# Expert queries from the loaded float32 weights instead of from split halves, in a two-block model with 512 row gathers

## The chip, the cores and the metric

The kernel runs on one core of a Trainium2 chip. The metric is the device time of one execution in microseconds (us), the median of three runs. Times inside an execution are us from the start of the profiled span.

## The reference, cut to what matters

Two transformer blocks over 256 tokens of width 2048 (one core, float32). The change sits in the last stage, the expert layer of the second block:

```python
def peer(x, wq, keys1, keys2, u, v):          # x is rmsnorm(x, g) of the stream
    q = (xf @ wq).reshape(t, PEER_HEADS, PEER_QDIM)        # 2048 x 2048 product, 8 heads
    s1 = jnp.einsum('thd,kd->thk', q[..., :half], keys1)   # 128 keys each
    s2 = jnp.einsum('thd,kd->thk', q[..., half:], keys2)
    v1, i1 = lax.top_k(s1, 16)
    v2, i2 = lax.top_k(s2, 16)
    ...                                       # the best 16 of the 16 x 16 sums: top_s, expert
    gate = jax.nn.softmax(top_s)
    z = jnp.einsum('cd,ced->ce', xc, u[ec])   # 128 rows of u for each token
    act = jax.nn.gelu(z) * gc
    return jnp.einsum('ce,ced->cd', act, v[ec])  # 128 rows of v for each token
```

Each token picks 8 heads x 16 experts = 128 rows of `u` and 128 of `v`, 8 KB each.

## The kernel before

**The steps.** All weight products of the model are one list of `Step`s that `run` walks in order. A weight tile of 1 MB (`raw`, 3 buffers, loaded on SP's queue by `load`) serves two steps. For each step ACT writes `hi` (the weights rounded to fp32r, `split_hi`) and DVE writes `lo` (the rest, `split_lo`), up to four steps ahead; the activations are held as a pair `hi`, `lo` as well (class `XT`). A step of `unit_B` then issues 16 matmuls: 8 of `hi` against both halves of the activations (512 columns), 8 of `lo` against `hi` (256 columns).

**The rest of the work** is written as generators. `pump()` runs once after each step and lets every living generator go on to its next `yield`; so the place of each vector instruction between the steps is fixed when the program is written, and each engine works through its own list in that order.

**The queries** (`e_q` weights, tile `eq`). Eight heads, four steps each, 32 steps. At a head's end `leave` sums the two halves on DVE (`eq_u`), `e_query` multiplies by 1/rms (`stE.R`, a row vector that `norm_end` makes), PE multiplies by the keys (`esc`), ACT copies (`es`), and `e_route` finds the top 16 on DVE (`route`, some 45 small instructions and three of 128x800), writes the indices into `keys_slots`, and makes the gates (an Exp on ACT). The heads of token tile 0 are routed first, one after the other, and a head's routing begins only when nearly all of the `u` gathers of the head before are issued.

**The gathers.** `e_stream` handles 512 items: for each token tile (2), head (8) and rank (16) a "U" (rows of `u`) and a "V" (rows of `v`). POOL issues an indirect DMA of 128 rows, 1.05 MB, into a free row buffer. A U item is then one DVE instruction over 128x2048 with an accumulated sum; a V item is four PE matmuls into `vacc` with a diagonal matrix `dg_ring` that ACT makes. In each `pump()` at most one waiting item is taken, and its buffer goes back for the next gather. V items begin when all eight heads' queries are made (`Ee["q"] == EH`). Until then there are three row buffers (`rows_a`, in the tile "xt1"); then `wide_rows` adds the three weight buffers (`rows_w`) and three quarters of the tile "xt0" that held the activations `xE` (`rows_x`); one quarter of each of the tiles "xt1" and "xt0" holds the gain times x for a token tile (`gain_rows`, its input from `f_g` through ACT's queue).

Of the kernel before, what the change touches and what calls it, by code (L numbers as in the profile page):

```python
# [20 lines left out]
P = 128  # L21
# [35 lines left out]
class Step:  # L57
    def __init__(self, src, mm, ready=None, post=None, row=None):
        self.src, self.mm, self.ready, self.post, self.row, self.pre = src, mm, ready, post, row, None
# [3 lines left out]
def tile_model(ctx: ExitStack, tc: tile.TileContext, x, xT, par, a_in, a_out, kv_in, kv_f, b_in, b_out,  # L63
# [95 lines left out]
    def run(steps):  # L159
# [6 lines left out]
        nd = NRAW  # L166
        for i, st in enumerate(steps):
            while nl < min(i + LOOK_SPLIT + 1, 2 * i + 2, n):
                while nh < min(nl + 2, n):
# [4 lines left out]
                if nl % 2 == 0 and 2 * nd < n:  # L174
                    load(nd, steps)
                    nd += 1
# [5 lines left out]
            st.mm(his.pop(i), los.pop(i))  # L182
# [88 lines left out]

    class Late:
# [76 lines left out]
    def resid_norm(st, chunks_ready, xt, wn):  # L349

        for c in range(4):
# [3 lines left out]
            norm_chunk(st, c)  # L355
        yield
# [26 lines left out]
    def unit_B(src, xt, cb, name, nk=KT, inter=False, per_sub=False):  # L383
# [27 lines left out]
        def leave(i):  # L411
            def f():
                if per_sub:
                    u = uo = w4(f"{name}_u{i}", (P, 2, T))
                else:
                    if "u" not in box:
                        box["u"] = w4(f"{name}_u", (P, 4, T))
                    u = box["u"]
                    uo = u[:, 2 * i:2 * i + 2, :]
                V.tensor_reduce(uo, box[i].rearrange("p j (a t) -> p j t a", a=2), axis=AX.X, op=OP.add)  # L420
                if per_sub:
                    spawn(cb(i)(u))
                elif i == 1:
# [3 lines left out]
        for n, (i, kg) in enumerate(order):  # L427
            st = Step(src(n // 2), mm(i, kg), ready=lambda kg=kg: xt.done() > kg)
            if kg == ng - 1:
                st.post = leave(i)  # L430
            steps.append(st)
# [826 lines left out]
    xtE = Late("xE", "xt0")  # L1258
# [4 lines left out]
    def e_setup():  # L1263
# [12 lines left out]
        rows.extend([r4[:, i, :] for i in range(1, 4)])  # L1276
        yield
# [7 lines left out]
    def e_query(h):  # L1285

        def f(q):
# [12 lines left out]
            if h:  # L1300
                yield
# [262 lines left out]
```

## Time and profile before

| | |
|---|---|
| median of three runs | 3056.84 us (3056.22 to 3057.11) |
| the profiled execution | 3057.23 us, span 3055.5 us |
| PE, DVE, ACT, POOL busy | 87%, 66%, 33%, 25% of the span |
| DMA | 840.90 MB, mean 275 GB/s |
| mean granted TensorE clock | 0.975 |

The share of busy time is a mean over stages. From about 1650 us the program is in the expert stage; the views of the trace below are of that stage. "Busy" of DMA is the mean over the core's 16 DMA engines. A wait is put down to the engine that released it.

### The profile page before, as it was taken

What the parts mean: (1) busy time and instruction counts of PE and PEld (TensorE: products, weight loads), DVE (VectorE), ACT (ScalarE), POOL (GpSimd) and SP (SyncE); (2) the same over time, 40 slices, a digit from 0 to 9 for tenths busy, and PEclk for the clock granted to TensorE, in tenths of its full rate; (3) what the DMA queues carried; (4) which work ended last, traced back from release to release, by engine and by line L of the source; (5) the groups of instructions that cost most, each with busy time, mean ns of one, the idle gap of its engine ahead of it and who ended that gap; (6) DMA issues with size and microseconds to landing.
All of it is one profiled execution on the core that took longest, in us unless ns stands there. A gap on an engine that the chain in (4) does not pass through costs nothing.

```text
span 3055.5 us, 30995 instructions
## 1 busy us (share of the span) xinstructions
PE 2659.7 (87%) x11252; PEld 1852.1 (61%) x11252; DVE 2006.1 (66%) x3088; ACT 1019.2 (33%) x1595; POOL 777.9 (25%) x612
## 2 busy tenths in 40 slices
PE   8999999999999999999999658777777777777766
PEld 7888888888888888888888543233332223322222
DVE  7978765656666568777766886555555565655454
ACT  6545544655554444555455211100111111110000
POOL 0412110000000000000000244555554444444553
PEclk9999999999999999999999778999999999999999
DMA  7444545444445454454555789999999999999997
GB/s 257 152 146 154 175 159 184 167 154 172 173 155 183 169 181 158 171 179 162 184 180 194 272 315 407 421 422 421 421 421 422 421 421 422 419 421 421 421 421 309
DMA packets 118521, 840.90 MB, mean 275 GB/s; under 512 B 13152, under 2 KB 13536, under 8 KB 17376
## 3 DMA queue, kind: packets, MB, share of 16 engines
q0 software_dynamic: 73728, 536.90, 42.5%
q1 hardware_dynamic: 43920, 298.73, 28.0%
q10 hardware_dynamic: 720, 3.28, 0.3%
q8 instruction: 89, 1.46, 0.2%
q14 instruction: 64, 0.52, 0.0%
HBM read 836.77 MB, written 2.10 MB: 275 GB/s over the span
## 4 chain that ended last, share of the span: by engine, by line
PE 55%; DMA 25%; DVE 11%; issue 7%; POOL 2%; ACT 0%; POOLq 0%; DVEq 0%; ACTq 0%
DMA rows_w<-in_e_v_dram,keys_slots 6%; PE vacc L1433 6%; DMA rows_a<-in_e_v_dram,keys_slots 5%; DMA rows_x<-in_e_v_dram,keys_slots 4%; DMA rows_a<-in_e_u_dram,keys_slots 3%; DMA rows_w<-in_e_u_dram,keys_slots 3%; DMA rows_x<-in_e_u_dram,keys_slots 2%; DVE rows_a L1415 2%; PE dq L406 2%; PE az L406 2%; PE aq L406 2%; PE da L406 2%; PE dx L406 1%; PE dr L406 1%; PE S L586 1%
## 5 line engine op out<-in xcount | busy, mean ns | idle before, releaser
L86 DVE TENSOR_TENSOR lo<-raw,hi 128x1024 fp32r<-128x1024 f32 x424 | 519.2, 1232 | 200.7 <-issue 24.1
L102 ACT ACTIVATE hi<-raw 128x1024 fp32r<-128x1024 f32 x424 | 444.2, 1057 | 475.2 <-PE az L406 55.2
L1433 PE MATMUL vacc<-rows_w,dg_ring 128*128 128x512 f32 x640 | 306.7, 625 | 111.0 <-DMA rows_w<-in_e_v_dram,keys_slots 77.6
L1433 PE MATMUL vacc<-rows_a,dg_ring 128*128 128x512 f32 x632 | 299.2, 619 | 112.2 <-DMA rows_a<-in_e_v_dram,keys_slots 90.1
L1433 PE MATMUL vacc<-rows_x,dg_ring 128*128 128x512 f32 x648 | 305.6, 617 | 104.6 <-DMA rows_x<-in_e_v_dram,keys_slots 82.3
L1433 PEld LDWEIGHTS vacc<-rows_w,dg_ring 128*128 128x128 f32 x640 | 121.2, 198 | 294.6 <-issue 225.0
L1433 PEld LDWEIGHTS vacc<-rows_x,dg_ring 128*128 128x128 f32 x648 | 120.9, 196 | 289.1 <-issue 226.8
L1433 PEld LDWEIGHTS vacc<-rows_a,dg_ring 128*128 128x128 f32 x632 | 118.7, 196 | 290.7 <-issue 238.4
L247 POOL TENSOR_TENSOR rq_y<-rq_m,mhalf 128x8 f32<-128x8 f32 (+2 forms) x24 | 31.6, 1318 | 889.3 <-DVE rq_m L95 889.0
L98 DVE SCALAR_TENSOR_TENSOR lo<-raw,prm,hi 128x512 fp32r<-128x512 f32 x256 | 178.8, 748 | 104.9 <-issue 60.7
L102 ACT ACTIVATE hi<-raw,prm 128x512 fp32r<-128x512 f32 x256 | 170.7, 717 | 121.4 <-PE bg L450 31.3
L1384 POOL DMA_INDIRECT rows_a<-in_e_u_dram,keys_slots x103 | 142.7, 1386 | 232.5 <-PE vacc L1433 123.4
L104 ACT ACTIVATE route<-route 128x16 f32<-128x16 f32 x16 | 3.5, 216 | 574.6 <-DVE route L93 574.6
L1415 DVE SCALAR_TENSOR_TENSOR rows_a<-rows_a,stE_r 128x2048 f32<-128x2048 f32 x60 | 140.7, 2348 | 70.6 <-DMA rows_a<-in_e_u_dram,keys_slots 70.6
L1415 DVE SCALAR_TENSOR_TENSOR rows_a<-rows_a,stE_r,rows_x 128x2048 f32<-128x2048 f32 x43 | 101.1, 2351 | 92.2 <-DMA rows_a<-in_e_u_dram,keys_slots 92.2
L1415 DVE SCALAR_TENSOR_TENSOR rows_x<-rows_x,stE_r 128x2048 f32<-128x2048 f32 x43 | 101.1, 2352 | 91.3 <-DMA rows_x<-in_e_u_dram,keys_slots 91.2
L1415 DVE SCALAR_TENSOR_TENSOR rows_w<-rows_w,stE_r,rows_x 128x2048 f32<-128x2048 f32 x42 | 98.7, 2351 | 85.7 <-DMA rows_w<-in_e_u_dram,keys_slots 85.5
L1384 POOL DMA_INDIRECT rows_w<-in_e_u_dram,keys_slots x77 | 115.1, 1495 | 139.6 <-PE vacc L1433 136.3
L1384 POOL DMA_INDIRECT rows_x<-in_e_u_dram,keys_slots x76 | 116.9, 1538 | 131.0 <-PE vacc L1433 126.7
L102 ACT ACTIVATE dg_ring<-ident,keys_slots 128x128 f32<-128x128 f32 x240 | 78.5, 389 | 185.7 <-PE vacc L1433 185.7
L102 ACT ACTIVATE keys_slots<-keys_slots 128x16 f32<-128x16 f32 x16 | 3.5, 216 | 387.6 <-DVE rows_w L1415 139.4
L1415 DVE SCALAR_TENSOR_TENSOR rows_w<-rows_w,stE_r,rows_a 128x2048 f32<-128x2048 f32 x35 | 82.3, 2351 | 66.3 <-DMA rows_w<-in_e_u_dram,keys_slots 66.3
(473 smaller groups left out, 6269.9 us busy)
## 6 DMA issues: line engine op xcount, KB each, us to landing
raw<-in_d_in_dram SPq DMA_DIRECT2D x76, 1024.0 KB, 4.9
raw<-in_a_in_dram SPq DMA_DIRECT2D x63, 1024.0 KB, 4.9
raw<-in_kv_in_dram SPq DMA_DIRECT2D x32, 1024.0 KB, 4.9
raw<-in_b_in_dram SPq DMA_DIRECT2D x32, 1024.0 KB, 4.9
raw<-in_a_out_dram SPq DMA_DIRECT2D x16, 1024.0 KB, 4.9
raw<-in_b_out_dram SPq DMA_DIRECT2D x16, 1024.0 KB, 4.9
raw<-in_d_out_dram SPq DMA_DIRECT2D x16, 1024.0 KB, 4.9
raw<-in_e_q_dram SPq DMA_DIRECT2D x16, 1024.0 KB, 4.9
```

The costliest lines, as they stand in the source:

```text
L86: V.tensor_tensor(o, a, b, op=op)
L98: V.scalar_tensor_tensor(o, a, s, b, op0=op0, op1=op1)
L102: S.activation(o, i, f, bias=bias, scale=scale)
L104: S.activation(o, i, f, bias=bias, scale=scale, accum_out=accum)
L247: G.tensor_tensor(y, m, mhalf[:, :w], op=OP.pow)
L406: PE.matmul(a[:, j, :], lhsT=h4[:, q, js], rhs=xt.both(kt), start=first, stop=last)
L586: PE.matmul(o, lhsT=lhs[:, h, sl], rhs=r, start=True, stop=True)
L1384: G.indirect_dma_start(out=dst, out_offset=None, in_=table, in_offset=bass.IndirectOffsetOnAxis(ap=Ee["idx"][:, gi, k:k + 1], axis=0))
L1415: V.scalar_tensor_tensor(r, r, stE.r[:, t:t + 1], Ee["xw", t], op0=OP.mult, op1=OP.mult, accum_out=Ee["z"][:, gi, k:k + 1])
L1433: PE.matmul(accs[t][c // 2][:, c % 2, :], lhsT=dg, rhs=r[:, c * 512:(c + 1) * 512], start=(j == 0), stop=last)
```

## The change

The 32 query steps become `plain`: PE multiplies the weights as loaded (float32) with float32 activations (class `XP`, which needs half the room), eight matmuls of 256 columns for each step (`unit_P`). Nothing is split for them, and a weight buffer is free when PE has done its second step. 1/rms is no longer multiplied into the queries: the order of the scores does not depend on it, and it enters as the scale of the gates' Exp. The query is copied out of PSUM by ACT. The two quarters of the tile "xt0" that the float32 activations leave free are row buffers from the start, so there are five until all queries are made.

```diff
@@ run
+            while nl < min(i + LOOK_SPLIT + 1, 2 * i + 2, n) and not steps[nl].plain:
...
+            if st.plain:
+                assert nl == nh == i or nl == n
+                st.mm(raw.pop(i))
+                freed(i)
+                nl = nh = i + 1
+            else:
+                st.mm(his.pop(i), los.pop(i))
@@ split4
+        if isinstance(xt, XP):
+            for q in range(4):
+                if q < 2:
+                    act(xt.x(k0 + q), ps[:, q, :], AF.Copy, scale=pcol(wn, wi + q))
+                else:
+                    ts(xt.x(k0 + q), ps[:, q, :], pcol(wn, wi + q), OP.mult)
@@ resid_norm
+        if isinstance(xt, XP):
+            norm_r(st)
+            st.done = True
+            return
@@ unit_P
+                for q in range(4):
+                    kt = kg * 4 + q
+                    for j in range(2):
+                        PE.matmul(box[i][:, j, :], lhsT=w4_[:, q, j * P:(j + 1) * P], rhs=xt.x(kt),
+                                  start=(kt == 0 and j == 0), stop=(kt == KT - 1 and j == 1))
@@ e_setup
         rows.extend([r4[:, i, :] for i in range(1, 4)])
+        rows.extend([xtE.get()[:, i, :] for i in (2, 3)])
@@ e_query
-            while not hasattr(stE, "done"):
-                yield
-            tt_(q, q, stE.R[:, None, :].to_broadcast([P, 2, T]), OP.mult)
-            yield
-            if h:
-                yield
+            q = w4(f"eq{h}", (P, 2, T))
+            act(q, acc, AF.Copy)
+            yield
@@ wide_rows
-        r4 = acts.tile([P, 4, D], F32, tag="xt0", name="rows_x")
-        gain_rows(1, r4[:, 0, :])
-        rows.extend([r4[:, i, :] for i in range(1, 4)])
+        gain_rows(1, xtE.get()[:, 0, :])
+        rows.append(xtE.get()[:, 1, :])
@@ e_route
+        while not hasattr(stE, "done"):
+            yield
         ts(tv, tv, tv[:, 0:1], OP.subtract)
-        act(tv, tv, AF.Exp, accum=sm)
+        act(tv, tv, AF.Exp, scale=stE.r[:, tt:tt + 1], accum=sm)
```

How instructions stand on POOL, from the first gather on, before:

```order
L1384 DMA rows_a<-in_e_u_dram,keys_slots 128x2048 x27
L1384 DMA rows_a<-in_e_v_dram,keys_slots 128x2048
L1384 DMA rows_w_14328<-in_e_u_dram,keys_slots 128x2048
L1384 DMA rows_w_14329<-in_e_v_dram,keys_slots 128x2048
L1384 DMA rows_w_14330<-in_e_u_dram,keys_slots 128x2048
```

And with the change (the last 11 gathers of `u` and the first V item; four more pairs of the first two rows, 20 gathers, stand ahead):

```order
L1443 DMA rows_a<-in_e_u_dram,keys_slots 128x2048 x3
L1443 DMA xE<-in_e_u_dram,keys_slots 128x2048 x2
L1443 DMA rows_a<-in_e_u_dram,keys_slots 128x2048 x3
L1443 DMA xE<-in_e_u_dram,keys_slots 128x2048 x2
L1443 DMA rows_a<-in_e_u_dram,keys_slots 128x2048
L1443 DMA rows_w_13958<-in_e_v_dram,keys_slots 128x2048
L1443 DMA rows_w_13959<-in_e_u_dram,keys_slots 128x2048
```

So 27 gathers of `u` stood ahead of the first gather into a wider buffer, and now 31 do; they take the three buffers `rows_a` and the two free quarters of `xE` in turn.

On DVE, in the middle of the query steps, before (the U items are the rows of L1415, the splits of weights the rows with `lo`):

```order
L86 TENSOR_TENSOR lo_13854<-raw_13681,hi_13821 128x1024
L420 TENSOR_REDUCE eq_u_13872<-eq_1_13739 128x512
L1415 SCALAR_TENSOR_TENSOR rows_a,keys_slots<-rows_a,stE_r 128x2048
L93 TENSOR_SCALAR route_0_13758<-route_0_13758 128x16
L86 TENSOR_TENSOR eq_u_13872<-eq_u_13872,stE_R 128x512
L86 TENSOR_TENSOR lo_13881<-raw_13681,hi_13852 128x1024
L1415 SCALAR_TENSOR_TENSOR rows_a,keys_slots<-rows_a,stE_r 128x2048
```

And at the same place of the second head's routing with the change (U items are the rows of L1476):

```order
L1430 CAST keys_slots<-route_0_13531 128x16
L1476 SCALAR_TENSOR_TENSOR rows_a,keys_slots<-rows_a,stE_r 128x2048
L94 TENSOR_SCALAR route_0_13531<-route_0_13531 128x16
L1476 SCALAR_TENSOR_TENSOR rows_a,keys_slots<-rows_a,stE_r 128x2048
L1438 RECIPROCAL route_0_13531<-route_0_13531 128x1
L94 TENSOR_SCALAR keys_slots<-route_0_13531 128x16
```

The splits, the sums and the products with 1/rms are gone from DVE's list; U items and routing are left.

On ACT, with the change, from the first query's copy on (`eq` is the query, `es` the scores, `route` the gates' Exp, which waits for DVE):

```order
L103 ACTIVATE eq_13403<-eq_0_13331 128x512
L103 ACTIVATE es_13419<-esc 128x512
L105 ACTIVATE route_0_13421<-route_0_13421,stE_r 128x16
L103 ACTIVATE eq_13498<-eq_1_13405 128x512
L103 ACTIVATE es_13419<-esc 128x512
L103 ACTIVATE eq_13594<-eq_0_13500 128x512
L105 ACTIVATE route_0_13531<-route_0_13531,stE_r 128x16
```

Before, 32 rows of `hi` stood among these. Now the copy of the second query stands right behind the Exp of the first head's gates, and the products with the keys (`esc`, PE) wait for that copy.

## Rows read from the trace of the kernel before

**Rows 1.** Windows by stage: busy time of each engine, granted clock, DMA share, GB/s.

```profile
core 0: us, PE busy (x) PEld busy (x) DVE busy (x) ACT busy (x) POOL busy (x), PEclk, DMA share, GB/s
1652.00:1684.00 32.00, 32.00 (x191) 28.12 (x191) 23.89 (x49) 14.64 (x21) 0.70 (x1) 1.00 0.49 180
1684.00:1812.00 128.00, 82.76 (x403) 70.86 (x401) 115.90 (x218) 24.86 (x35) 34.96 (x27) 0.80 0.75 280
1812.00:1860.00 48.00, 28.82 (x56) 12.40 (x57) 32.87 (x71) 5.93 (x17) 26.41 (x21) 0.76 0.98 398
1860.00:2440.00 580.00, 437.32 (x930) 174.16 (x929) 340.50 (x596) 57.56 (x149) 295.05 (x234) 0.97 1.01 422
...
2480.00:3020.00 540.00, 395.97 (x840) 156.60 (x839) 300.58 (x424) 47.25 (x129) 274.35 (x216) 0.97 1.01 421
```

**Rows 2.** Waits between 1690 and 1812 us: total, times, longest, in us.

```profile
ACT route L104 <- DVE route L93: 50.5, 3, 17.6
...
PE esc L1297 <- DVE eq_u L86: 34.4, 6, 12.3
```

**Rows 3.** POOL in order of time: the first U gather, the first V gather.

```profile
1692.05 1.19 POOL L1384 DMA_INDIRECT rows_a<-in_e_u_dram,keys_slots  x1 [21.15 <-DVE keys_slots L1373]
...
1812.16 0.94 POOL L1384 DMA_INDIRECT rows_a<-in_e_v_dram,keys_slots  x1 [1.74 <-DMA rows_x<-in_f_g_dram]
```

**Rows 4.** Groups by tile in the query stage: ns min/median/max, first and last start.

```profile
L86 DVE TENSOR_TENSOR lo<-raw,hi x34: 1203/1218/1272, 1639.4 to 1789.8; 128x1024 fp32r<-128x1024 f32 x34
...
L133 SPq DMA_DIRECT2D raw<-in_e_q_dram x8: 327/328/328, 1683.8 to 1766.1; - x8
...
L420 DVE TENSOR_REDUCE eq_u<-eq x8: 1211/1219/1225, 1668.6 to 1798.2; 128x512 f32<-128x1024 f32 x8
...
L102 ACT ACTIVATE es<-esc x8: 571/588/599, 1677.9 to 1806.1; 128x512 f32<-128x512 f32 x8
```

**Rows 5.** PE in order of time: query step, key products, V products, one late key product.

```profile
1652.94 0.39 PE L406 MATMUL eq<-xE,hi 128*128 128x512 f32 x1
...
1676.77 1.05 PE L1297 MATMUL esc<-keys_slots,eq_u 128*128 128x128 f32 x8
1677.58 0.48 PE L406 MATMUL eq<-xE,hi 128*128 128x512 f32 x1
...
1707.72 0.55 PE L1297 MATMUL esc<-keys_slots,eq_u 128*128 128x128 f32 x1 [12.28 <-DVE eq_u L86]
...
2003.24 3.67 PE L1433 MATMUL vacc<-rows_a,dg_ring 128*128 128x512 f32 x8 [1.30 <-DMA rows_a<-in_e_v_dram,keys_slots]
```

**Rows 6.** DVE in order of time: the first head's routing and the first U item.

```profile
1678.49 0.29 DVE L1327 MAX8 route<-es 128x8 f32<-128x128 f32 x1
...
1681.92 0.67 DVE L86 TENSOR_TENSOR eq_u<-eq_u,stE_R 128x512 f32<-128x512 f32 x1
...
1683.64 0.17 DVE L1352 CAST route<-route 128x32 f32<-128x32 uint32 x1
...
1686.71 1.23 DVE L86 TENSOR_TENSOR lo<-raw,hi 128x1024 fp32r<-128x1024 f32 x1
1687.85 0.98 DVE L86 TENSOR_TENSOR eq<-keys_slots,route 128x800 f32<-128x800 f32 x1
...
1691.00 1.22 DVE L86 TENSOR_TENSOR lo<-raw,hi 128x1024 fp32r<-128x1024 f32 x1
1699.54 2.35 DVE L1415 SCALAR_TENSOR_TENSOR rows_a<-rows_a,stE_r 128x2048 f32<-128x2048 f32 x1 [7.32 <-DMA rows_a<-in_e_u_dram,keys_slots]
```

**Rows 7.** DVE in order of time: two U items back to back.

```profile
1793.18 2.35 DVE L1415 SCALAR_TENSOR_TENSOR rows_a<-rows_a,stE_r 128x2048 f32<-128x2048 f32 x1
...
1795.45 2.35 DVE L1415 SCALAR_TENSOR_TENSOR rows_a<-rows_a,stE_r 128x2048 f32<-128x2048 f32 x1
```

**Rows 8.** A window of ten us after PE's long wait, columns as in rows 1.

```profile
1700.00:1710.00 10.00, 2.28 (x10) 2.31 (x11) 9.96 (x12) 4.78 (x8) 2.76 (x2) 0.50 0.81 298
```

**Rows 9.** The chain that ended last, in order of time: the second gain row's load.

```profile
1806.07 10.71 DMA rows_x<-in_f_g_dram
```

More of the change, by code (lines that the diff above doesn't have):

```diff
@@ L57, with __init__ @@
 class Step:
-    def __init__(self, src, mm, ready=None, post=None, row=None):
+    def __init__(self, src, mm, ready=None, post=None, row=None, plain=False):
+        self.plain = plain
         self.src, self.mm, self.ready, self.post, self.row, self.pre = src, mm, ready, post, row, None
@@ L166, in run, with freed @@
         nd = NRAW
+        def freed(i):
+            nonlocal nd
+            if i % 2 and 2 * nd < n:
+                load(nd, steps)
+                nd += 1
         for i, st in enumerate(steps):
-            while nl < min(i + LOOK_SPLIT + 1, 2 * i + 2, n):
-                while nh < min(nl + 2, n):
+            while nl < min(i + LOOK_SPLIT + 1, 2 * i + 2, n) and not steps[nl].plain:
+                while nh < min(nl + 2, n) and not steps[nh].plain:
                     split_hi(nh, steps)
@@ L173, in run @@
                 nl += 1
-                if nl % 2 == 0 and 2 * nd < n:
-                    load(nd, steps)
-                    nd += 1
+                freed(nl - 1)
             if st.pre is not None:
@@ L270, in done, with __init__, get, x @@
             return self.n
+    class XP:
+        def __init__(self, name, tag):
+            self.name, self.tag, self.buf, self.n = name, tag, None, 0
+        def get(self):
+            if self.buf is None:
+                self.buf = acts.tile([P, 4, D], F32, tag=self.tag, name=self.name)
+            return self.buf
+        def x(self, kt):
+            return self.get()[:, kt // 8, kt % 8 * T:(kt % 8 + 1) * T]
+        def done(self):
+            return self.n
     class Late:
@@ L412, in f @@
             def f():
[L413 to L423, printed above, removed]
+                if "u" not in box:
+                    box["u"] = w4(f"{name}_u", (P, 4, T))
+                V.tensor_reduce(box["u"][:, 2 * i:2 * i + 2, :], box[i].rearrange("p j (a t) -> p j t a", a=2), axis=AX.X, op=OP.add)
+                if i == 1:
                     spawn(cb(box.pop("u")))
@@ L430, in unit_B, with unit_P, mm, f @@
                 st.post = leave(i)
+            steps.append(st)
+        return steps
+    def unit_P(src, xt, cbs, name):
+        box = {}
+        steps = []
+        def mm(i, kg):
+            def f(w):
+                if kg == 0:
+                    box[i] = acc_tile(f"{name}_{i}")[:, 0, :].rearrange("p (j t) -> p j t", t=T)
+                w4_ = w.rearrange("p (q n) -> p q n", n=T)
+                for q in range(4):
[3 more added lines that the diff above has]
+                                  start=(kt == 0 and j == 0), stop=(kt == KT - 1 and j == 1))
+            return f
+        for n in range(8):
+            i, kg = n // 4, n % 4
+            st = Step(src(n // 2), mm(i, kg), ready=lambda kg=kg: xt.done() > kg, plain=True)
+            if kg == 3:
+                st.post = lambda i=i: spawn(cbs(i)(box.pop(i)))
             steps.append(st)
@@ L1411, in e_stream @@
                 continue
+            while not hasattr(stE, "done"):
+                yield
             (kind, gi, k), r = pend.pop(0)
```

16 lines of the change are left out of this document (9 added, 7 removed).

## The prediction

> **What bounds the kernel now.** I read the windows by stage first. From 1860 us to 3020 us the DMA engines are busy without a gap at 421 to 422 GB/s, while PE is busy for 437 of 580 us and DVE for 341 [rows 1]: the gather stream is the bound there. An item moves 128 x 2048 x 4 bytes = 1.049 MB, so an item costs 1.049/0.4215 = 2.49 us, and 512 of them 1274 us, four tenths of the kernel. That part is not touched by the change. What it can touch is when the stream begins to fill the DMA engines. Between 1684 and 1812 us they moved only 280 GB/s, between 1812 and 1860 us 398 [rows 1]. In time of a full stream that is (421 - 280) x 128/421 = 42.9 us and (421 - 398) x 48/421 = 2.6 us of unused capacity. Every byte moved there shortens the end one for one, since nothing after 1860 us is idle.
>
> Why is it unused? In that stretch DVE is busy for 115.9 of 128 us and PE for 82.8 [rows 1]. The list of waits says who is late: PE's key products wait 34.4 us for the queries on DVE, and ACT's Exp 50.5 us for routing on DVE [rows 2]. DVE's order holds splits, sums, routing and U items in one line, and with three row buffers, each held until its U item has had its turn on DVE, no more than three gathers can be out.
>
> **What the change removes.** From DVE: 32 splits of 1.22 us, 8 sums of 1.22 us [rows 4] and 8 products with 1/rms of some 0.6 us (1681.92 to 1683.64 holds one and a split, less 1.14 [rows 6]), 39 + 10 + 5 = 54 us. From ACT: the 32 `hi` copies, which PE's products waited for in turn; a query's copy of about 0.59 us takes their place, by the `es` copy of the same shape [rows 4].
>
> **What it adds on PE.** The trace holds no float32 product of 256 columns, but it holds 128 and 512. Four key products are recorded as eight instructions of 128 columns and take 1677.58 - 1676.77 = 0.81 us [rows 5], 0.79 ns a column. Four V products, eight of 512 columns, take 3.67 us with their drain [rows 5], 0.90 ns a column. A new step is eight products, 16 instructions of 256 columns: 3.24 to 3.67 us. I take 3.44, the middle. An old step was 16 matmuls at 32.00/191 us [rows 1] = 2.68 us. So 32 steps grow by 32 x 0.76 = 24 us (18 to 32 us). This lies behind DVE and the DMA engines, since PE had 45 idle us in that stretch [rows 1]; what it costs without that cover is in the rivals.
>
> **When the first gather goes.** The first query product still starts at 1652.9 us [rows 5]; PE was full up to there and its list ahead is the same. Four steps and the transposes for the last quarter of the activations (0.9 us): head 0 is ready at 1667.6. Copy 0.6, the next step 3.4, key products 0.8, copy 0.6: DVE begins routing at 1672.5 instead of 1678.49. Routing took until 1691.00, with a split and a product (1.72 us) and another split (1.14) within [rows 6]: 9.65 us remain, so the indices are there at 1682.2 and the first gather goes 1.05 us later as before [rows 3, 6], at **1683.2 us, 8.9 us earlier** than 1692.05. Its U item follows 7.5 us behind (1692.05 to 1699.54 [rows 3, 6]), at 1690.7.
>
> **The query stage after that.** DVE has U items of 2.27 us (back to back [rows 7]) and a head's routing of 9.65 us and about 0.5 us for the gates. The order gives 26 U items and three more routings until the gain row of the second token tile: 26 x 2.27 + 3 x 10.2 = 90 us, so until 1781 us if no gather is late. PE: 32 x 3.44 + 8 x 0.8 + 0.9 = 117 us from 1652.9, so 1770 without a wait. One wait is certain: head 1's query is ready at 1682.2 but its copy stands on ACT behind the Exp of head 0, which waits on DVE for the first U item (1693.0). PE runs one more step to 1685.6 and then stands until about 1694, **8.4 us**. After the 12.28 us wait before 1707.72 [rows 5] the granted clock was 0.50 for the next ten us [rows 8]; I take 2.5 us for that and 3 us for later waits on the Exp and Gelu: the last query at **1784 us** (its scores' copy starts at 1806.1 before [rows 4]), and the first V gather soon after instead of at 1812.16 [rows 3].
>
> **The sum, in DMA time.** The stretch from 1684 us has 42.9 us to win. Two weight loads move into it: before, eight of the 16 `e_q` loads were issued from 1683.8 us on [rows 4], since splits run ahead and free the buffers early. With the change three loads go ahead and one more for each two finished steps, six landed by then, so ten are left: 2 x 2.49 = 5.0 us more. 37.9 us remain if the engines are never idle. They will be at first: until about 1743 us PE frees seven buffers and DVE has taken some 15 gathers, 22 x 2.49 = 54.8 of 59 us, 4 us lost. Another 3 us I put down as an estimate for short spells with one transfer out, since one alone takes 7.46 us to its U item [rows 3, 6]. From then to the last query more is asked for than 421 GB/s: a U item every 2.27 us and a load every 7 us. All that may be issued ahead of the last query is 31 gathers and ten loads, 41 x 2.49 + 7 = 109 us from 1684: enough work until 1793, so the end of the queries at 1784 is covered with 9 us to spare. The 2.6 us between 1812 and 1860 I leave where they are, as the order there is the same.
>
> Gain 42.9 - 5.0 - 7 = **31 us**. Span 3055.5 - 31, and the 1.7 us outside it: 3026.2; the median of the runs is 0.4 us below the profiled time, so **3026 us**. The bounds: never idle gives 38, with the 2.6 us 41, hence 3016; lost capacity of 20 us instead of 7 (15 of the 1684 to 1743 stretch left idle and a dip twice as deep) gives 18, hence 3039.
>
> A page would make it less: the Trainium skill (DMA: Bandwidth & Descriptors, Specifications) gives about 358 GB/s as what one core gets of the memory. By it, less of the capacity in the query stage would be unused: (358 - 280) x 128/358 = 28 us, less 5.9 and 7, a gain of 15 and 3042 us. The trace disagrees with that sentence: 421 to 422 GB/s hold for 1120 us [rows 1], and a chance of 0.01 is enough for it.
>
> **The rivals.** (1) *PE's waits on ACT take DVE's place.* ACT's order puts the copies of four queries behind an Exp or a Gelu that waits for DVE, and these waits were up to 17.6 us long [rows 2]. If each of the four holds PE by 8 to 12 us, not only the first, the last query comes at 1808 to 1820, 15 to 27 us after the issued work has run dry: gain 4 to 16, **3041 to 3053 us**. Against it: DVE reaches the second and third Exp sooner without the splits, by then PE has four steps, 13.8 us, between copies. Chance 0.12.
> (2) *Slower: PE is held at half clock.* Granted 0.50 [rows 8] is the 1.2 GHz level. A step then takes 6.9 us, and the query stage is what the V items and the wide buffers wait for. Beyond 1793 us each us is lost; the gain of 31 is used up when the last query comes at 1824, 40 us late, which is 12 of the 32 steps at half clock. With 16 steps: 55 us, 3057 + 15 = **3072**; with all, 3126. For it: PE has more and longer waits than in the model's body. Against it: from 1860 us on PE works in bursts between waits (75% busy) and the clock is 0.97 [rows 1]. A float32 product of 256 columns that cost 40% more than both neighbours would do the same. Chance 0.10. The Trainium skill (TensorE: Matmul & The Clock Gate, What's actually happening) says that the throttled state is the default and activity releases it; the row after the long wait agrees, 0.50.
> (3) *Weight loads come late.* The gain row's 1 MB took 10.71 us with gathers out [rows 9]; a freed buffer is wanted again 13.8 us later. With five gathers ahead of it a load takes 6 x 2.49 = 15 us, so 1.2 us for each of ten loads, 12 us: the last query at 1796, 3 us past the cover, **3029 us**; within the main case.
> (4) *No change*: the gathers come earlier but the saturated stream is paced by something else, or the wider stage starts with as much idle time as it saved. PE and DVE with a quarter and more idle there [rows 1] speak against it; 3057, chance 0.05.
> (5) More than 41 us, below 3016, would need an earlier first gather than worked out: 0.03.
>
> **How the numbers follow.** Main case 0.70, 3016 to 3039. Two tenths stay outside 3014 to 3048: the slow rival, no change, and the far end of (1). A measurement of this kernel tells about 0.2% (6 us) from no change. Faster: 0.70 + 0.03 + 0.11 = 0.84; same 0.06; slower 0.10.
>
> **What the profile after would show.** Right: the first gather of `u` near 1683; DVE without `lo` in the stage; 31 gathers ahead of the first V; the window from 1684 to 1784 near 400 GB/s; a last query near 1784; a PE wait of some 8 us for ACT's second query copy. Wrong: a query step much longer than 3.7 us at full clock, granted clock near 0.5 for most of the stage, or GB/s from 1790 to 1860 that falls well below 398.

## The result, and the profile after

| | before | after |
|---|---|---|
| median | 3056.9 us (3056.22 to 3057.22, 5 runs) | **3022.7 us** (3021.95 to 3024.83, 5 runs) |
| ratio | | 0.9889, 95% interval 0.9875 to 0.9904 |
| span of the profiled execution | 3055.5 us | 3020.9 us |

The kernel is 34.2 us faster; 3026 us had been forecast, with 3014 to 3048 as range. The windows by stage of the changed kernel (columns as in rows 1; the last line is the ten us behind the end of PE's one long wait in the query stage):

```profile
1640.00:1684.00 44.00, 44.00 (x211) 38.12 (x210) 16.96 (x60) 4.85 (x11) 0.70 (x1) 1.00 0.41 147
1684.00:1784.00 100.00, 91.50 (x435) 80.36 (x433) 81.03 (x179) 10.23 (x21) 44.19 (x30) 0.95 0.99 402
1784.00:1812.00 28.00, 8.63 (x19) 3.90 (x18) 26.50 (x50) 6.41 (x15) 20.57 (x12) 0.66 1.00 398
1812.00:1860.00 48.00, 38.71 (x82) 15.87 (x82) 32.36 (x72) 5.53 (x12) 28.12 (x22) 0.93 1.01 422
1860.00:2440.00 580.00, 439.26 (x930) 174.68 (x929) 338.78 (x596) 54.94 (x145) 293.50 (x232) 0.97 1.01 421
...
1695.14:1705.14 10.00, 10.00 (x38) 8.71 (x39) 9.69 (x29) 0.60 (x1) 5.49 (x4) 0.72 1.02 427
```

The last number of a line, the GB/s, is what to read. Where the engines moved 280 GB/s between 1684 and 1812 [rows 1], they now move 402 and 398; from 1860 us on nothing has changed. PE has become the busy engine of the query stage (91.5 of 100 us), and DVE has room there (81.0).

The waits between 1684 and 1812 us, which answer to [rows 2] (total, times, longest):

```profile
ACT route L105 <- DVE route L94: 44.7, 4, 20.0
...
DVE rows_a L1476 <- DMA rows_a<-in_e_u_dram,keys_slots: 14.4, 6, 7.5
...
PE esc L1357 <- ACT eq L103: 8.5, 2, 7.8
...
DVE xE L1476 <- DMA xE<-in_e_u_dram,keys_slots: 2.7, 2, 2.0
```

PE's 34.4 us of waiting for DVE are gone; ACT's Exp waits for DVE as it did. POOL, PE, DVE and ACT in order of time, as [rows 3, 5, 6]:

```profile
1685.15 1.15 POOL L1443 DMA_INDIRECT rows_a<-in_e_u_dram,keys_slots  x1 [17.76 <-DVE keys_slots L1430]
...
1789.15 1.45 POOL L1443 DMA_INDIRECT rows_a<-in_e_u_dram,keys_slots  x1 [4.38 <-DVE rows_a L1476]
1790.91 0.94 POOL L1443 DMA_INDIRECT rows_w<-in_e_v_dram,keys_slots  x1 [0.31 <-issue]
```

```profile
1654.37 3.61 PE L484 MATMUL eq<-xE,raw 128*128 128x256 f32 x16
...
1658.69 13.98 PE L484 MATMUL eq<-xE,raw 128*128 128x256 f32 x64
1672.51 1.05 PE L1357 MATMUL esc<-keys_slots,eq 128*128 128x128 f32 x8
...
1695.14 2.08 PE L1357 MATMUL esc<-keys_slots,eq 128*128 128x128 f32 x8 [7.76 <-ACT eq L103]
1697.01 15.84 PE L484 MATMUL eq<-xE,raw 128*128 128x256 f32 x64
...
1783.67 1.16 PE L1357 MATMUL esc<-keys_slots,eq 128*128 128x128 f32 x8 [0.75 <-ACT eq L103]
1799.01 2.90 PE L1494 MATMUL vacc<-rows_w,dg_ring 128*128 128x512 f32 x3 [14.17 <-DMA rows_w<-in_e_v_dram,keys_slots]
```

```profile
1674.23 0.29 DVE L1384 MAX8 route<-es 128x8 f32<-128x128 f32 x1 [6.04 <-ACT es L103]
...
1684.02 0.17 DVE L1430 CAST keys_slots<-route 128x16 uint32<-128x16 f32 x1
1691.66 2.35 DVE L1476 SCALAR_TENSOR_TENSOR rows_a<-rows_a,stE_r 128x2048 f32<-128x2048 f32 x1 [7.47 <-DMA rows_a<-in_e_u_dram,keys_slots]
...
1792.95 2.29 DVE L90 TENSOR_TENSOR xE<-xs,xE 128x2048 f32<-128x2048 f32 x1 [0.91 <-DMA xE<-in_f_g_dram]
```

```profile
1673.60 0.60 ACT L103 ACTIVATE es<-esc 128x512 f32<-128x512 f32 x1 [3.75 <-PE esc L1357]
1694.20 0.31 ACT L105 ACTIVATE route<-route,stE_r 128x16 f32<-128x16 f32 x1 [20.00 <-DVE route L94]
...
1694.51 0.58 ACT L103 ACTIVATE eq<-eq 128x512 f32<-128x512 f32 x1
```

PE's one long wait before the last query is explained by the last block, ACT's: the second query's copy (1694.51) stood on ACT behind an Exp that waited 20.00 us for DVE, and DVE had stood 7.47 us at the first U item.

**The ledger.** What a stretch loses in stream time is its length times (1 - GB/s / 421.5), with 421.5 GB/s as the rate of the full stream. The windows of the kernel before that [rows 1] does not have:

```profile
1640.00:1684.00 44.00, 44.00 (x244) 38.07 (x243) 29.39 (x54) 19.56 (x26) 0.70 (x1) 1.00 0.52 193
1684.00:1784.00 100.00, 68.41 (x334) 58.79 (x332) 90.91 (x195) 22.09 (x31) 23.40 (x19) 0.81 0.75 276
1784.00:1812.00 28.00, 14.36 (x71) 12.06 (x69) 24.98 (x24) 2.77 (x4) 11.56 (x8) 0.75 0.78 293
```

Over the windows 1640 to 1684, 1684 to 1784, 1784 to 1812 and 1812 to 1860 the kernel before lost 23.9, 34.5, 8.5 and 2.7 us, together 69.6; the changed one 28.7, 4.6, 1.6 and 0, together 34.9. The difference, 34.7 us, is the 34.6 us between the spans. The ledger is bookkeeping from the traces: it tells where time was lost, not why. The same sum for every other kernel of this study (all times but the median from its profile, in us):

| kernel | median | first U gather | last key products | first V gather | first V product | lost 1640 to 1684, and in the three windows behind |
|---|---|---|---|---|---|---|
| before | 3056.9 | 1692.05 | 1803.99 | 1812.16 | 1821.88 | 23.9; 34.5, 8.5, 2.7 |
| after | 3022.7 | 1685.15 | 1783.67 | 1790.91 | 1799.01 | 28.7; 4.6, 1.6, 0 |
| e1 three buffers | 3040.5 | 1685.24 | 1794.44 | 1795.62 | 1822.34 | 28.7; 15.3, 2.6, 8.0 |
| e2 busy DVE | 3047.1 | 1685.31 | 1796.82 | 1814.36 | 1822.70 | 29.3; 18.9, 7.4, 4.2 |
| e5 1/rms in the query | 3045.8 | 1695.51 | 1792.42 | 1794.91 | 1821.62 | 28.6; 18.1, 1.6, 10.3 |
| e4 four extra products | 3060.5 | 1685.16 | 1823.04 | 1801.45 | 1838.25 | 28.7; 17.4, 5.9, 21.2 |
| e3 one extra product | 3031.1 | 1682.34 | 1790.88 | 1790.39 | 1807.12 | 29.4; 5.1, 8.2, 1.1 |
| e13 as e4, gain row early | 3046.9 | 1683.97 | 1822.35 | 1800.76 | 1826.20 | 28.9; 14.4, 6.5, 10.3 |
| e6 loads ahead | 3022.3 | 1684.91 | 1783.90 | 1782.45 | 1801.13 | 17.5; 11.0, 6.5, 0.7 |
| e8 late Exp | 3019.8 | 1684.47 | 1776.18 | 1786.99 | 1795.20 | 28.8; 1.1, 1.8, 0 |
| e9 both | 3014.5 | 1683.62 | 1776.77 | 1782.84 | 1791.15 | 17.8; 9.4, 0.2, 0.1 |

The losses account for the span of each within 1.3 us, but for e3: 8.9 us more lost than after, a span 5.7 us longer, since its execution reached the expert stage 2.8 us sooner. Such starts differ between executions: in e11, the changed kernel again, the first U gather goes at 1683.62.

### The profile page after: what moved, and what is told of

Its sections match the earlier page's. It is cut to its first block, busy times and chain, and to the rows that moved or that the text cites. A ratio compares the mean times of both kernels' runs of the same rounds, so it can differ in the third digit from the quotient of the medians.

```text
span 3020.9 us, 30853 instructions
## 1 busy us (share of the span) xinstructions
PE 2673.7 (89%) x11250; PEld 1863.0 (62%) x11250; DVE 1951.8 (65%) x3029; ACT 990.7 (33%) x1562; POOL 792.4 (26%) x612
## 4 chain that ended last, share of the span: by engine, by line
PE 54%; DMA 26%; DVE 9%; issue 7%; POOL 3%; ACT 0%; SPq 0%; POOLq 0%; DVEq 0%; ACTq 0%
DMA rows_w<-in_e_v_dram,keys_slots 7%; DMA xE<-in_e_v_dram,keys_slots 6%; DMA rows_a<-in_e_v_dram,keys_slots 6%; PE vacc L1494 5%; DMA rows_a<-in_e_u_dram,keys_slots 3%; DMA rows_w<-in_e_u_dram,keys_slots 2%; PE dq L450 2%; PE az L450 2%; DMA xE<-in_e_u_dram,keys_slots 2%; PE da L450 2%; PE dx L450 1%; PE dr L450 1%; DVE rows_a L1476 1%; PE aq L450 1%; DVE xE L1476 1%
## 5 line engine op out<-in xcount | busy, mean ns | idle before, releaser
L87 DVE TENSOR_TENSOR lo<-raw,hi 128x1024 fp32r<-128x1024 f32 x392 | 480.0, 1232 | 197.7 <-PE ao L511 23.9
L103 ACT ACTIVATE hi<-raw 128x1024 fp32r<-128x1024 f32 x392 | 411.3, 1058 | 437.0 <-PE az L450 51.4
L1494 PE MATMUL vacc<-xE,dg_ring 128*128 128x512 f32 x640 | 302.1, 616 | 94.0 <-DMA xE<-in_e_v_dram,keys_slots 77.1
L1494 PEld LDWEIGHTS vacc<-xE,dg_ring 128*128 128x128 f32 x640 | 119.3, 195 | 274.7 <-issue 219.3
L103 ACT ACTIVATE hi<-raw,prm 128x512 fp32r<-128x512 f32 x256 | 170.6, 717 | 121.1 <-PE bg L512 31.2
L1476 DVE SCALAR_TENSOR_TENSOR rows_a<-rows_a,stE_r 128x2048 f32<-128x2048 f32 x51 | 119.8, 2349 | 75.5 <-DMA rows_a<-in_e_u_dram,keys_slots 75.5
L1443 POOL DMA_INDIRECT xE<-in_e_u_dram,keys_slots x87 | 123.5, 1419 | 152.4 <-PE vacc L1494 120.3
L1476 DVE SCALAR_TENSOR_TENSOR xE<-xE,stE_r 128x2048 f32<-128x2048 f32 x43 | 101.1, 2351 | 94.2 <-DMA xE<-in_e_u_dram,keys_slots 94.2
L1476 DVE SCALAR_TENSOR_TENSOR rows_a<-rows_a,stE_r,xE 128x2048 f32<-128x2048 f32 x43 | 101.1, 2351 | 92.4 <-DMA rows_a<-in_e_u_dram,keys_slots 92.4
L1476 DVE SCALAR_TENSOR_TENSOR rows_w<-rows_w,stE_r,xE 128x2048 f32<-128x2048 f32 x42 | 98.7, 2351 | 86.0 <-DMA rows_w<-in_e_u_dram,keys_slots 86.0
L1476 DVE SCALAR_TENSOR_TENSOR xE<-xE,stE_r,rows_a 128x2048 f32<-128x2048 f32 x44 | 103.2, 2349 | 60.4 <-DMA xE<-in_e_u_dram,keys_slots 60.3
```

The costliest lines, as they stand in the source:

```text
L87: V.tensor_tensor(o, a, b, op=op)
L103: S.activation(o, i, f, bias=bias, scale=scale)
L1443: G.indirect_dma_start(out=dst, out_offset=None, in_=table, in_offset=bass.IndirectOffsetOnAxis(ap=Ee["idx"][:, gi, k:k + 1], axis=0))
L1476: V.scalar_tensor_tensor(r, r, stE.r[:, t:t + 1], Ee["xw", t], op0=OP.mult, op1=OP.mult, accum_out=Ee["z"][:, gi, k:k + 1])
L1494: PE.matmul(accs[t][c // 2][:, c % 2, :], lhsT=dg, rhs=r[:, c * 512:(c + 1) * 512], start=(j == 0), stop=last)
```

## The experiments

My theory: the gain is stream time that lay idle in the query stage, opened by DVE's relief and the two extra buffers together, and PE's longer products are covered. All edits are on the changed kernel.

**e1: three buffers.**

```diff
-        rows.extend([xtE.get()[:, i, :] for i in (2, 3)])
...
-        rows.append(xtE.get()[:, 1, :])
+        rows.extend([xtE.get()[:, i, :] for i in (1, 2, 3)])
```

> The changed kernel with three row buffers instead of five until the last query is made (quarters 2 and 3 of xE join the ring together with quarter 1, at the end of the queries); nothing else is changed. My theory: both the relieved VectorE and the two extra buffers open the DMA engines in the query stage. One row's turn, with the changed kernel's landing time of about 7.5 us and a U product of 2.27 us and about 1 us to issue the next gather, is 10.8 us, so three buffers give a row each 3.6 us, against 3.35 us with five (31 gathers in 104 us): the first V gather at 1797 to 1810 instead of 1791, lost stream time between 1684 and there 10 to 20 us instead of 6, time 3027 to 3037 us. Rival, the buffers are everything: the gain goes but for a few us, 3049 to 3057 us, and the first V gather stays near 1812. Rival, the buffers do nothing and VectorE's relief is everything: 3021 to 3025 us.

Measured: 3040.54 us, ratio 0.9943 (0.9926 to 0.9959). Half of the gain is gone; neither rival holds, and my own range was 3.5 us short. The first V gather came sooner than I had said: only 29 U gathers stand ahead of it, not 31. What I had left out is in PE's order:

```profile
1750.56 1.65 PE L1356 MATMUL esc<-keys_slots,eq 128*128 128x128 f32 x6 [8.03 <-ACT eq L103]
...
1794.44 1.16 PE L1356 MATMUL esc<-keys_slots,eq 128*128 128x128 f32 x8 [0.69 <-ACT eq L103]
1822.34 1.22 PE L1493 MATMUL vacc<-rows_w,dg_ring 128*128 128x512 f32 x1 [26.74 <-ACT dg_ring L103]
```

A second 8 us wait for a query copy (rival 1's mechanism, with DVE late), and 27.9 us between the last key products and the first V product, where the changed kernel has 15.3. In that gap the diagonal stands on ACT behind an Exp, ahead of which ACT waits 24.07 us for DVE; the gap holds row buffers, and 1812 to 1860 loses 8.0 us.

**e2: five buffers, DVE loaded.** Results of the extra instructions are not read. There are 40 of them, 40 x 1.22 = 49 us, against the 54 us that the change took from DVE.

```diff
+    def extra(i):
+        l = wpool.tile([P, 2, 512], F32R, tag="lo", bufs=LOOK_SPLIT + 1, name=f"extra{i}")
+        tt_(l.rearrange("p a n -> p (a n)"), xs[0][:, :1024], xs[1][:, :1024], OP.subtract)
...
                 st.mm(raw.pop(i))
+                extra(i)
+                if i % 4 == 3:
+                    extra(i + 1000)
```

> The changed kernel (five row buffers, plain float32 queries) with 40 extra VectorE subtracts of 128x1024, of the size of the removed lo splits and eq_u sums, whose results nobody reads: one after each query step and a second after every fourth. About 36 of them, 36 x 1.22 = 44 us, fall behind 1684, so VectorE has 81 + 44 = 125 us of work in a stage where it had 81 us in 100. My theory (VectorE's relief is needed for the gain): the 31st U gather comes about 20 us later than 1789, some 9 us of that had been spare or is filled by V gathers, time 3035 to 3048 us; PE's wait for VectorE does not come back, since no query waits for VectorE. Rival, five buffers are enough whatever VectorE does: 3021 to 3026 us. Rival, VectorE's relief is everything: 3050 to 3057 us.

Measured: 3047.1 us, 0.9967 (0.9954 to 0.9979); as expected but for one point. The 31st U gather goes 23 us late:

```profile
1812.61 1.45 POOL L1450 DMA_INDIRECT rows_a<-in_e_u_dram,keys_slots  x1 [4.38 <-DVE rows_a L1483]
```

PE's waits did come back, through ACT: 20.8 us for query copies in four waits, where I had said that no query waits for DVE. Of the gain of 34 us, DVE's load takes 24 and the two buffers 18: each part needs the other.

**e5: 1/rms back in the query.**

```diff
-            norm_r(st)
-            st.done = True
+            yield
+            yield from norm_end(st)
...
             act(q, acc, AF.Copy)
+            while not hasattr(stE, "done"):
+                yield
+            tt_(q, q, stE.R[:, None, :].to_broadcast([P, 2, T]), OP.mult)
...
-        act(tv, tv, AF.Exp, scale=stE.r[:, tt:tt + 1], accum=sm)
+        act(tv, tv, AF.Exp, accum=sm)
```

> The changed kernel with one of its parts undone: 1/rms is multiplied into every query on VectorE again, behind the norm's broadcast, and Exp has no scale; the plain float32 products and the five row buffers stay. My theory: the first query waits for the norm (some 6 to 10 us), the first U gather comes at 1691 to 1697 instead of 1685, PE waits for VectorE again (10 to 25 us in all, since VectorE's multiply stands in order behind U products that wait for gathers), the last query comes at 1795 to 1810; time 3030 to 3042 us. Rival, the late 1/rms is worth nothing because the query stage's end is covered: 3021 to 3026 us. Rival, it is most of the gain: 3045 to 3057 us.

Measured: 3045.82 us, 0.9962 (0.9947 to 0.9976): outside my range, at the lower end of "most of the gain". The first gather (1695.51), PE's waits for DVE (14.8 us) and the last query (1792.42, even sooner) were as expected; the price was not. Two things add to it. Only 27 U gathers lie ahead of the first V gather, not 31; and the changeover is long again, by ACT's order:

```profile
1793.62 0.60 ACT L103 ACTIVATE es<-esc 128x512 f32<-128x512 f32 x1 [1.97 <-PE esc L1360]
1793.63 0.34 ACTq L1344 DMA_DIRECT2D xE<-in_f_g_dram  x1
1794.23 1.28 ACT L105 ACT_TABLE_LOAD   x1
1820.97 0.22 ACT L105 ACTIVATE route<-route 128x16 f32<-128x16 f32 x1 [25.45 <-DVE route L94]
...
1821.18 1.55 ACT L103 ACTIVATE dg_ring<-ident,keys_slots 128x128 f32<-128x128 f32 x5
```

Behind the last scores ACT takes an Exp before the first diagonal for a V item, and that Exp waits 25.45 us for DVE. So this part of the change, by the prediction's estimate 5 us of DVE's work, is worth 23 of the 34 us: what counts is where the product stands in DVE's order, and the first gather that goes 10.4 us later. That the two things make up the whole price is read from the trace, not tried. No run gave ACT its 32 `hi` copies back or PE its old steps; these two parts are not priced by themselves.

**e4: PE made longer by 41.5 us.** The products are extra and unread.

```diff
+                    box["x"] = full[:, 1, :T]
...
+                if name != "eq0":
+                    for q in range(4):
+                        PE.matmul(box["x"], lhsT=w4_[:, q, :P], rhs=xt.x(kg * 4 + q), start=True, stop=True)
```

> The changed kernel with four extra plain float32 products of 128x128x256 in each of the last 24 query steps (from the second unit on), into an unused half of the unit's PSUM tile that nobody reads: 96 x 0.432 = 41.5 us more PE work, so that the last query comes at about 1825 instead of 1784. My theory (PE's end of the queries is covered by the U stream, with 5 to 9 us to spare, and beyond that it costs one for one, less what the stream still moves): 3045 to 3058 us. Rival, PE's length counts one for one from the start: 3062 to 3066 us. Rival, the stream before 1860 is no bound at all and the later stages take it up: under 3035 us.

Measured: 3060.54 us, 1.0008 (0.9999 to 1.0018), 2.5 us above my range and 1.5 below that of the rival that counts PE's length from the start. The last key products came 39.4 us later, the span is 38.1 us longer: next to nothing is covered. This speaks against the prediction's 9 us to spare. DVE shows where the rows stand, PE what follows:

```profile
1832.77 2.29 DVE L90 TENSOR_TENSOR xE<-xs,xE 128x2048 f32<-128x2048 f32 x1 [33.92 <-DMA xE<-in_f_g_dram]
```

```profile
1823.04 1.16 PE L1362 MATMUL esc<-keys_slots,eq 128*128 128x128 f32 x8 [0.75 <-ACT eq L103]
1838.25 2.07 PE L1499 MATMUL vacc<-rows_w,dg_ring 128*128 128x512 f32 x2 [14.05 <-ACT dg_ring L103]
```

DVE stands for 33.92 us at the second token tile's product with the gain row. Its load goes into a quarter of `xE`, which the last query's first steps read, and it stands in ACT's order behind the copy of the last scores: it is issued at 1824.24. All U items behind it in DVE's order stand too, and their buffers with them.

In the middle of the stage there is a second effect, the reverse of rival 1:

```profile
1765.72 0.18 DVE L90 TENSOR_TENSOR keys_slots<-keys_slots 128x16 f32<-128x16 f32 x1 [13.34 <-ACT keys_slots L103]
```

```profile
1768.44 2.81 POOL L1448 DMA_INDIRECT rows_a<-in_e_u_dram,keys_slots  x1 [14.02 <-DVE rows_a L1481]
```

DVE's product of a head's Gelu with its gates waits 13.34 us for the Gelu, which stands in ACT's order behind copies of a query and its scores that wait for PE's longer steps; POOL's next gather waits 14.02 us for DVE. Before 1784 the stream loses 12.8 us more than in the changed kernel, so not all of the 38 us are paid at the end of the queries.

**e3: PE made longer by 10.4 us** (the same edit with `range(1)`).

> As the run with four extra products a step, but with one: one extra float32 product of 128x128x256 in each of the last 24 query steps, 24 x 0.432 = 10.4 us more PE work, its result unread. In that run the last query moved by 39.4 us and the span by 38.1 us, so hardly anything covered PE's end; with 31 U gathers before the first V gather there as in the changed kernel. Theory one for one (the number of U gathers before the last query is fixed by the order of the program, about one a query step, so a longer step starves the stream): 3029 to 3033 us. Theory of the prediction (about 9 us of stream work cover PE's end): 3022 to 3026 us.

Measured: 3031.13 us (3028.31 to 3031.41), 0.9918 (0.9902 to 0.9935): 8.4 us for 10.4, within the theory of one for one; hardly covered. Here the loss lies behind 1784 (8.2 us from there to 1812, where the changed kernel loses 1.6), beside DVE's wait for the gain row:

```profile
1801.63 2.29 DVE L90 TENSOR_TENSOR xE<-xs,xE 128x2048 f32<-128x2048 f32 x1 [10.09 <-DMA xE<-in_f_g_dram]
```

**e13: e4 with the gain row loaded early.** Two buffers of the `hi` splits are empty then and take the row in two halves; DVE multiplies each half on its own.

```diff
+    def load_gain():
+        a = len(g_ahead)
+        t = wpool.tile([P, 2, 512], F32R, tag="hi", bufs=LOOK_SPLIT + 2, name=f"gain{a}")
+        t = t.rearrange("p a n -> p (a n)").bitcast(F32)
+        nc.sync.dma_start(t, f_g[1:2, a * 1024:(a + 1) * 1024].to_broadcast([P, 1024]))
+        g_ahead.append(t)
...
+                if n - i in (14, 12):
+                    load_gain()
...
+                mul(o[:, c], xs[t][:, c], g_ahead.pop(0))
```

> As the run with four extra products a query step, but the second token tile's gain row (1 MB) is loaded before the last query, into two empty buffers of the hi splits, instead of behind it. In the run without this, the row's load was issued behind the last query's scores at 1824.2, VectorE's product with it and the U products and the gate behind that product came some 12 us later, and with them the first V product at 1838.3; all row buffers stood full meanwhile. If this chain is why PE's end is paid one for one: the first V product 8 to 12 us sooner against the last query, 3049 to 3054 us instead of 3060.5. If PE's end itself is what is paid: 3058 to 3062 us.

Measured: 3046.86 us, 0.9967 (0.9955 to 0.998), 13.7 us less than e4 at the same end of the queries (1822.35), and 2 us below my range. DVE's product needs only PE to have read the quarter (the second half goes at 1811.28, where e4 issued its load at 1824.24), and the first V product follows the last scores in 3.9 us instead of 15.2:

```profile
1811.28 1.23 DVE L90 TENSOR_TENSOR xE<-xs,gain 128x1024 f32<-128x1024 f32 x1 [4.85 <-PE eq L500]
```

```profile
1822.35 1.16 PE L1377 MATMUL esc<-keys_slots,eq 128*128 128x128 f32 x8 [0.75 <-ACT eq L103]
1826.20 4.63 PE L1514 MATMUL vacc<-rows_w,dg_ring 128*128 128x512 f32 x5 [2.69 <-ACT dg_ring L103]
```

So 13.7 of the 38 us that the late last query cost were the chain behind it: gain row, product, U item, gate, diagonal. The stage still loses 31.2 us behind 1684, 25.0 more than the changed kernel: 9.8 of them before 1784, where DVE waits 13.34 us for the Gelu as in e4, the rest behind it. That wait was not taken away in a run, so its price is not shown.

**e6: more loads ahead.** The `hi` and `lo` buffers take query weights, a ring of 14 steps; `load_ahead` loads one step's half of a weight tile, and `p0` is the first query step.

```diff
...
+            k = i - p0 + 14
...
+            if k % 14 >= 6:
+                load_ahead(k, "hi" if k % 2 == 0 else "lo")
+            elif k % 2:
+                load((p0 + k) // 2, steps)
```

> The changed kernel with more of the query weights loaded ahead: the buffers of the hi and lo splits, which stand empty once the last split step is done, take query weights too (a ring of 14 steps instead of 6), so that about 22 of the 32 steps' weights are issued before 1684, when the DMA engines ran at 132 GB/s, and about five loads of 1 MB fewer lie behind 1684; nothing is left out. Theory bytes (the stage from 1684 is bound by the DMA engines): 5 x 2.49 = 12 us faster than the changed kernel, 3010 to 3014 us. Theory order (31 U gathers and the last query's end at about 1784 are fixed by the order of the program and by PE, and the first V gather cannot come before it): the DMA engines go idle instead, 3019 to 3024 us.

Measured: 3022.26 us, 0.9891 (0.9874 to 0.9907): no change, as the theory of order has it. The windows show the bytes moved ahead and the idle time that took their place (147 GB/s in the first in the changed kernel):

```profile
1640.00:1684.00 44.00, 44.00 (x211) 38.14 (x210) 17.15 (x61) 4.60 (x11) 0.69 (x1) 1.00 0.67 254
1684.00:1784.00 100.00, 90.72 (x432) 79.70 (x430) 88.45 (x206) 10.24 (x21) 55.45 (x33) 0.95 0.95 375
1784.00:1812.00 28.00, 7.41 (x16) 3.29 (x16) 16.33 (x16) 3.85 (x6) 12.81 (x8) 0.66 0.81 323
```

11.2 us won before 1684, 12.0 lost behind. One detail of that theory was wrong: the first V gather did come sooner, at 1782.45, but its product only at 1801.13, behind ACT's Exp, behind DVE's wait for the gain row:

```profile
1795.64 2.29 DVE L90 TENSOR_TENSOR xE<-xs,xE 128x2048 f32<-128x2048 f32 x1 [12.05 <-DMA xE<-in_f_g_dram]
```

**e8: the gate's part of the routing eight turns later.**

```diff
+        def gate():
+            for _ in range(8):
+                yield
+            ts(tv, tv, tv[:, 0:1], OP.subtract)
+            act(tv, tv, AF.Exp, scale=stE.r[:, tt:tt + 1], accum=sm)
...
+        spawn(gate())
```

> The changed kernel with the gate's part of the routing (the subtraction, Exp with the scale 1/rms, the division) issued eight turns of the helper tasks later, so that ScalarE does not stand at an Exp that waits for VectorE while the next query's copy is queued behind it; nothing is left out. In the changed kernel that Exp waited 44.7 us in four waits in 1684 to 1812, and PE 7.8 us for the second query's copy behind it, after which its clock was 0.53 for 10 us. Expected by my theory: PE's wait goes from 7.8 to under 1 us, the last query comes at 1773 to 1776 instead of 1784, and the stream, which had only 4.6 us to spare before 1784, gives 1 to 5 us: 3018 to 3022 us. Rival, PE's end sets the time one for one: 3011 to 3015 us. Rival, PE waits at the next point in order just as long: 3022 to 3025 us.

Measured: 3019.75 us (3018.13 to 3020.84), 0.9882 (0.9866 to 0.9899). PE's wait of 7.76 us before the second query's key products is gone, later ones are 1.9 and 0.7 us, and the last key products come 7.5 us sooner. Of the 6.2 us that were lost behind 1684 it wins 3.3, as my theory had it. By the times alone the gain is not clear: the intervals of the two ratios overlap.

```profile
1686.53 1.05 PE L1357 MATMUL esc<-keys_slots,eq 128*128 128x128 f32 x8
```

**e9: both edits.**

> The changed kernel with both: query weights loaded ahead into the empty split buffers, and the gate's part of the routing issued eight turns later; nothing is left out. If the stage has two limits of nearly one length, the DMA engines (41 items of 2.49 us, 102 us from 1684) and PE (100 us), each single edit gives little and both together give about 8 to 11 us: 3011 to 3015 us. If the bytes alone are the limit: 3010 to 3014 us here and in the run with the loads ahead alone. If a third limit is next (31 U products and the routing on VectorE, 81 us of work before 1784, in order): 3016 to 3022 us.

Measured: 3014.45 us (3012.82 to 3016.72), 0.9864 (0.9848 to 0.9881): no gain for e6, 3 us for e8, 8 us for both. I read it so: single edits move only one of two limits of nearly one length, the stream's bytes and PE's end.

**e11 and e10.** The changed kernel again, and e9 with `range(12)`, on one chip.

> The changed kernel itself, unaltered, on the same chip as the next run, so that the two can be compared directly: 3021 to 3025 us, first U gather near 1685, 31 U gathers before the first V gather near 1791.

> As the run with both edits (query weights loaded ahead into the empty split buffers, the gate's part of the routing later), but the gate's part twelve turns later instead of eight; nothing is left out. In that run the Exp still waited 38.2 us for VectorE and PE 3.3 and 1.6 us for query copies behind it. If those waits are still worth time: PE's waits under 2 us in all, 3009 to 3013 us. If VectorE's order is the limit now (the 31st U gather waits there for a row's U product): 3013 to 3016 us, the same as with eight. In both cases 7 to 13 us below the changed kernel on this chip.

Measured: 3023.37 us (3020.55 to 3024.84), 0.9895 (0.9879 to 0.9912), and 3015.1 us (3014.18 to 3016.15), 0.9868 (0.9851 to 0.9884): with both edits the kernel is 8.3 us below the changed one on the same chip, and four more turns bring nothing.

**e12: e9 with the gain row early.**

> As the run with both edits (query weights loaded ahead, gate eight turns later), and the second token tile's gain row loaded before the last query into two buffers of the hi splits that are empty by then; nothing is left out. That run lost 9.7 us of stream time between 1684 and 1860, nearly all before 1784, where five buffers and the order on VectorE set the pace. If what it lost hangs on the changeover behind the last query: 3008 to 3012 us. If it was lost before, as the windows say: 3013 to 3016 us, and VectorE's wait for the gain row is gone all the same.

Measured: 3015.66 us (3014.23 to 3017.2), 0.9867 (0.9851 to 0.9883): the same as e9, as the windows had said. DVE's wait for the gain row, 1.39 us in e9, is gone. e9 loses its 9.4 us before 1784, and there POOL waits for DVE. The last U gather of e9 ahead of the V gathers, and its window:

```profile
1781.09 1.44 POOL L1474 DMA_INDIRECT rows_a<-in_e_u_dram,keys_slots  x1 [4.38 <-DVE rows_a L1507]
```

```profile
1684.00:1784.00 100.00, 88.32 (x433) 77.36 (x431) 88.22 (x206) 12.98 (x24) 49.60 (x32) 0.98 0.96 382
```

That DVE's order is the limit in e9 is read from these waits, not tried.

## Why the prediction was right, and where it was not

**The bound: right.** The ledger of unused stream time is the whole of the gain, and it holds for the other kernels of the table. The stream holds 421 to 422 GB/s again; the figure of about 358 GB/s that the Trainium skill states as the limit of one core (DMA: Bandwidth & Descriptors, Specifications), and the 3042 us by it, do not fit this kernel, which runs on one core.

**The price on PE: right.** A step is 16 instructions of 256 columns; four steps took 1672.51 - 1658.69 = 13.82 us, 3.455 us a step against 3.44. The middle between the neighbours in [rows 5] was a guess that came out.

**The first gather: 1685.15 against 1683.2.** 1.4 of the 2.0 us come from the first query product, at 1654.37 where I had kept 1652.94. That is this execution and not the change: in e11 it comes at 1652.85, and the first gather at 1683.62. From head 0 on, the forecast's terms add up to 5.4 us where 4.9 were counted; the first copy runs beside the next step. The routing took 1684.02 - 1674.23 = 9.79 us against 9.65.

**PE's waits and last query: right, in part by luck.** 7.76 us for the second query's copy (8.4 forecast). The clock behind the long wait had been misread: the window of [rows 8] begins 7.72 us before the wait ends, at 1707.72. In the ten us behind it the clock before was 0.76, not 0.50:

```profile
1707.72:1717.72 10.00, 10.00 (x47) 8.93 (x48) 9.72 (x21) 1.66 (x2) 1.00 (x2) 0.76 0.86 314
```

In the changed kernel it was 0.72. The key products there took 2.08 us instead of 1.05 and the next 64 instructions 15.84 instead of 13.98, together 2.9 us (2.5 forecast); then 0.75 us of waits, not 3. Last copy at 1783.02, forecast 1784: the waits are 2.5 us shorter in all, the start was 1.4 us later.

**DVE's sum: too short.** The second gain row's product was to come at 1781 "if no gather is late". DVE got to it at 1792.95 - 0.91 = 1792.04: its first U item came 1.0 us later, and behind that item it waited 14.4 - 7.5 + 2.7 = 9.6 us for rows. It cost next to nothing, since the DMA engines were full while DVE waited:

```profile
1743.00:1784.00 41.00, 40.25 (x197) 35.36 (x195) 30.73 (x47) 5.08 (x8) 16.80 (x13) 1.00 1.01 419
```

**The sum.** Loads moved behind 1684: 28.7 - 23.9 = 4.8 us lost more ahead of it, against 5.0. Idle time between 1684 and 1812: 4.6 + 1.6 = 6.2, against 7. The 2.6 us between 1812 and 1860, which I left where they were, are gone: the first V product comes at 1799.01 now, ahead of that window, and not at 1821.88 within it, and I take the dip to have belonged to their start. These terms give 42.9 - 4.8 - 6.2 + 2.6 = 34.5; the mis-sized term is the dip, 2.6 of the 3.7 us by which the forecast of the span was short.

**The step that failed** changed no number of the forecast, but would have in another kernel: "the end of the queries at 1784 is covered with 9 us to spare". I had counted the gathers that may be issued and divided by the stream's rate. e3 and e4 show a cover of 1 to 2 us, no more than the runs of one kernel differ by; and in e8 an end 7.5 us sooner won 3.3 us of stream time, so that some of the end at 1784 seems to have lain bare already. The last query's end is not where the V items begin: a chain follows, 15.3 us here, through the first V row's landing, the gain row's load, DVE's order and ACT's order, and meanwhile row buffers stand full. In the changed kernel it happened to lie beside DVE's routing (the gain row made DVE wait 0.91 us); 10 us later it lay bare (10.09 us in e3). And longer steps starve the stream ahead of the end too, as DVE's 13.34 us in e4 show. By that cover, rival 2's break-even at a last query of 1824 was right by luck: e4 had it at 1823 and came out level with before.

**The rivals.** (1) PE held by ACT: one such wait, not four, since DVE reached the later Exps in time; e1 and e2, where DVE is late or its buffers few, brought the second one of 8.03 and 9.3 us. The mechanism was right, its condition is DVE's lag. (2) Half clock: 0.95 from 1684 to 1784; not seen. (3) Late loads: they landed in 9.2 us (median of ten), under the 13.8 us in which they were wanted. (4) No change and (5) more than 41 us: not so.

## What to carry to other kernels

Where a later stage is bound by a stream that never stops, keep a ledger of the stream's unused time ahead of it: from the trace of a run it accounts for the price of each edit here within 1.3 us, e3 excepted. A cover is not the work that could be issued; it ends where a row buffer has to be given back (e3, e4, e13), so follow one buffer through the changeover, with every engine's order, before calling anything hidden. Two limits of nearly one length hide each other: loads ahead alone gave nothing, the late Exp alone some 3 us, both together 8.

## What the runs showed of the hardware

PE's clock did not suffer from being the busy engine with float32 products: 1.00 from 1784 to 1812 in e4, where PE never stopped, against 0.66 in the changed kernel, where it worked 8.6 of 28 us. The window of e4:

```profile
1784.00:1812.00 28.00, 28.00 (x140) 24.85 (x139) 14.30 (x54) 1.79 (x3) 5.73 (x5) 1.00 0.81 332
```

The Trainium skill (TensorE: Matmul & The Clock Gate, What's actually happening) has the throttled state as the default that activity releases; these two windows agree.

The same 1 MB load of query weights landed in 4.8 us (median) before 1684 and in 9.2 us with gathers beside it.
